# W_down's third product added in PSUM onto the fifth's sum, in a decoder layer on one core

## The chip, the core and the metric

The kernel runs on one core of one Trainium2 chip. TensorE (PE) multiplies into PSUM, VectorE (DVE) and ScalarE (ACT) work on what lies in PSUM and SBUF, GpSimd (POOL) does small things, and SyncE (SP) issues the transfers. The metric is the device time of one execution in microseconds, as the median of several runs.

## What is computed

One layer of a decoder: 512 tokens of width 1024 in fp32, with attention and convolution ahead (not touched here), then the MLP and a gated projection. Of the reference, this is the part in question:

```python
h = rms_norm(x, g_pre_mlp[i])
f = jnp.square(jax.nn.relu(h @ w_up[i])) @ w_down[i]
x = x + rms_norm(f, g_post_mlp[i])
ple_gate = jax.nn.sigmoid(rms_norm(x, g_ple[i]) @ w_ple_gate[i])
x = x + ple_gate * (p[i] @ w_ple_proj[i])
```

## The kernel before

Every fp32 operand is split into a high and a low part by `split` (lines 63 to 66: an ACT cast for the high part, a DVE subtraction for the low one), and every product is three matmuls (`mm3`, lines 90 to 93: high by high, high by low, low by high). One matmul is 128 by 128 by 512 columns.

W_down is multiplied by Strassen's method in Winograd's form: tokens are cut in an upper half (blocks 0 and 1 of 128 tokens) and a lower half (blocks 2 and 3), output columns in two halves of 512, and seven products of half size take the place of eight. They run in the order `ORDER = (1, 2, 6, 7, 5, 3, 4)`. Each product has eight tiles of weights (`i` from 0 to 7); for each tile TensorE does both token blocks `t` of a half, two slices of 128 each, so six matmuls for block 0 and then six for block 1. A sum sits in one PSUM bank per block, `acc[n, t]`. Products 6 and 5 go on in the banks of product 1 (their matmuls don't start a new sum), product 4 in those of product 7; products 1, 2, 7 and 3 start in fresh banks. There are eight banks.

At the end of a product's last tile, `done(n, t)` (lines 782 to 798) brings the sum into the column buffers `cx`, four of 128 by 1024 in SBUF: `cx[t]` for the upper tokens and `cx[t + 2]` for the lower ones. After product 5 it makes two copies of the same bank on ACT (lines 792 and 793), and the sum of product 7 and the first copy on DVE (line 794); after product 3 it adds product 3's bank to the second copy on DVE (line 796).

When a row of `cx` is complete, `chain2(t)` calls `residual1` (lines 531 to 537): the square sum of the row on ACT (`rstd_of`, L125, with an accumulator read), the row sum plus epsilon on DVE (L129), the power -1/2 on POOL (L133), the scaling by it and by the gain on DVE (L533), the addition to the residual `x` (L534), then square sum, power and scaling again for the next norm (L536). `turn(t)` transposes that row on TensorE (L141) for the gate projection. The table `AFTER` says behind which tile of which product these steps are written: block 0's chain behind product 3's last tile, block 1's behind tile 1 of product 4, block 0's transposes behind tile 5 of product 4, block 1's after the last.

TensorE and SP run in the order in which the code is written; ACT, DVE and POOL in an order that a scheduler sets by priority when the program is built, and each then runs its own list strictly in that order. The loads of the tiles (L739) are written three tiles ahead of their use, into four raw buffers; the split halves take two buffers each of a pool of 15, which also holds `cx`, the two gains (L118) and the rows that wait for their transposes. A load waits until the raw buffer's last reader, a DVE subtraction, is done. The loads of W_ple_gate (L807) for the projection share the raw buffers with the last tiles of product 4.

Of the kernel before, what the change touches and what calls it, by code (L numbers as in the profile page):

```python
# [12 lines left out]
ALU = mybir.AluOpType  # L13
# [11 lines left out]
NJ = FF // P // 2  # L25
# [8 lines left out]
def hybrid_block(ctx, tc, x, p, g_pre_mix, w_in, b_gate, w_conv, w_attn_out, w_conv_out, w_o,  # L34
                 g_post_mix, g_pre_mlp, w_up, w_down, g_post_mlp, g_ple, w_ple_gate, w_ple_proj, out):
    nc = tc.nc
# [3 lines left out]
    p = p[0]  # L40
# [13 lines left out]
    def bigt(shape, dt=F32R, name="big"):  # L54
        return big.tile(shape, dt, tag="big", name=name)

    def bank():
        return psp.tile([P, 512], F32, tag="ps", name="ps")
# [21 lines left out]
    def w4(dt=F32):  # L80
        return wts.tile([P, 2, 512], dt, tag="w", name="w4")
# [8 lines left out]
    def mm3(ps, lh, ll, rh, rl, start, stop, onto=False):  # L90
        nc.tensor.matmul(ps, lh, rh, start=start, stop=False, skip_group_check=onto)  # L91
        nc.tensor.matmul(ps, lh, rl, start=False, stop=False, skip_group_check=onto)  # L92
        nc.tensor.matmul(ps, ll, rh, start=False, stop=stop, skip_group_check=onto)  # L93
# [27 lines left out]
    def rstd_of(parts):  # L121
        ss = []
        for a in parts:
            s = sml.tile([P, 1], F32, tag="ss", name="ss")
            nc.scalar.activation(junk[:, 0:a.shape[-1]], a, AF.Square, scale=1.0 / 32.0, accum_out=s)  # L125
            ss.append(s)
        m = sml.tile([P, 1], F32, tag="ms", name="ms")
        if len(ss) == 1:
            nc.vector.tensor_scalar(m, ss[0], EPS, None, op0=ALU.add)  # L129
        else:  # L130
            nc.vector.scalar_tensor_tensor(m, ss[0], EPS, ss[1], op0=ALU.add, op1=ALU.add)
        r = sml.tile([P, 1], F32, tag="rs", name="rs")
        nc.gpsimd.tensor_tensor(r, m, mhalf, op=ALU.pow)  # L133
        return r
# [134 lines left out]
    for t in range(2, NT):  # L269
        ps = bank()  # L270
# [197 lines left out]
    for j in range(NK):  # L468
# [24 lines left out]
        if j == 7:  # L493
            for kk in range(2):
                ps = bank()
# [5 lines left out]
    def rows(nk, stat, w, tail, chain):  # L501
# [19 lines left out]
        for t in range(NT):  # L521
# [6 lines left out]
                    mm3(acc[t, hf], sh[:, tok], sl[:, tok], wk[0][:, cs], wk[1][:, cs], False, k == nk - 1)  # L528
            chain(t, [acc[t, 0], acc[t, 1]])

    def residual1(xt, c, gpost, gnext):
        r = rstd_of([c])
        nc.vector.scalar_tensor_tensor(c, c, r, gpost, op0=ALU.mult, op1=ALU.mult)  # L533
        nc.vector.tensor_tensor(xt, xt, c, op=ALU.add)  # L534
        r2 = rstd_of([xt])
        nc.vector.scalar_tensor_tensor(c, xt, r2, gnext, op0=ALU.mult, op1=ALU.mult)  # L536
        return [c[:, 0:512], c[:, 512:1024]]
# [21 lines left out]
    hf = [bigt([P, 2, 4, 256], F32, "hf") for _ in range(2)]  # L559
# [24 lines left out]
    for t in range(NT):  # L584
        tok = slice(t * P, (t + 1) * P)
        for h_ in range(2):
            cs = slice(h_ * 512, (h_ + 1) * 512)
            ps = bank()
# [142 lines left out]
    def load_t(n, i):  # L731
        raw = raws.tile([P, 2, 512], F32, tag="raw", name="raw")
        if n in RIGHT:
            r, c = RIGHT[n]
            r0 = r * FF // 2 + i * 2 * P
            src = w_down[r0:r0 + 2 * P, c * 512:(c + 1) * 512].rearrange("(k p) n -> p k n", p=P)
        else:
            src = wsum[i][:, MADE[n]]
        nc.sync.dma_start(raw, src)  # L739
        lo, hi = w4(F32R), w4(F32R)  # L740
        split(hi, lo, raw)
        for u in range(2):
            tiles[n, 2 * i + u] = hi[:, u], lo[:, u]

    def load_s(n, g):
        if (n, g) == (1, 0):
            hi, lo = (wts.tile([P, 4, 256], F32R, tag="w", name="s0") for _ in range(2))
        else:
            both = bigt([P, 2, 4, 256], name="sb")
            hi, lo = both[:, 0], both[:, 1]  # L750
        split(hi, lo, quarter(*LEFT[n], g))
        for v in range(4):
            stat[n, 4 * g + v] = hi[:, v], lo[:, v]
        a11, a12 = quarter(0, 0, g), quarter(0, 1, g)
        if n == 1:
            nc.vector.tensor_tensor(a11, quarter(1, 0, g), a11, op=ALU.subtract)
        elif n == 2:
            nc.vector.tensor_tensor(a12, a12, a11, op=ALU.subtract)
        elif n == 6:
            nc.vector.tensor_tensor(a11, quarter(1, 1, g), a11, op=ALU.subtract)  # L760

    back = {}
    xr2 = lambda t: back['x', t // 2][:, t % 2, :]
# [9 lines left out]
    cx = {}  # L773
    hn2 = {}
    h3 = []
    acc = {}

    def chain2(t):
        hn2[t] = residual1(xr2(t), cx[t].rearrange("p a b -> p (a b)"), *back["g"])

    def done(n, t):
        ps = acc[n, t]
        if n == 1:
            cx[t] = w4()
            cx[t + 2] = w4()
            nc.scalar.copy(cx[t][:, 0], ps)
        elif n == 2:
            nc.vector.tensor_tensor(cx[t][:, 0], ps, cx[t][:, 0], op=ALU.add)
        elif n == 6:
            nc.scalar.copy(cx[t + 2][:, 0], ps)  # L790
        elif n == 5:
            nc.scalar.copy(cx[t + 2][:, 1], ps)
            nc.scalar.copy(cx[t][:, 1], ps)
            nc.vector.tensor_tensor(cx[t + 2][:, 1], acc[7, t], cx[t + 2][:, 1], op=ALU.add)
        elif n == 3:
            nc.vector.tensor_tensor(cx[t][:, 1], ps, cx[t][:, 1], op=ALU.add)
        elif n == 4:
            nc.vector.tensor_tensor(cx[t + 2][:, 0], ps, cx[t + 2][:, 0], op=ALU.add)

# [10 lines left out]
    def turn(t):  # L810
        if not h3:
# [3 lines left out]
    plan_t = [(n, i) for n in ORDER for i in range(NI)]  # L815
    plan_s = [(n, g) for n in ORDER for g in range(4)]
    AFTER = {(7, 0): lambda: reload('x', x1s), (5, 6): gains, (4, 6): lambda: reload('p', pps), (3, 7): lambda: chain2(0), (4, 1): lambda: chain2(1), (4, 2): lambda: load_pg(0),
             (4, 4): lambda: load_pg(2), (4, 5): lambda: turn(0)}
    nt = ns = 0
    for n, i in plan_t:  # L820
        while ns < min(len(plan_s), plan_s.index((n, i // 2)) + 3):
            load_s(*plan_s[ns])
            ns += 1
        while nt < min(len(plan_t), plan_t.index((n, i)) + 4):
            load_t(*plan_t[nt])
            nt += 1
        for t in range(2):
            if i == 0:
                acc[n, t] = acc[{6: 1, 5: 6, 4: 7}[n], t] if n in (6, 5, 4) else bank()
            ts = slice(t * P, (t + 1) * P)  # L830
            for j in (2 * i, 2 * i + 1):
                sh, sl = stat[n, j]
                th, tl = tiles[n, j]
                mm3(acc[n, t], sh[:, ts], sl[:, ts], th, tl, j == 0 and n in (1, 2, 7, 3),
                    j == NJ - 1, n in (6, 5, 4))
            if i == NI - 1:
                done(n, t)
        if (n, i) in AFTER:
            AFTER[n, i]()
    turn(1)  # L840
    for t in range(2, NT):
        chain2(t)
        for k in range(2 * t, 2 * t + 2):
            pgw[k] = wrow(w_pg, k)
# [29 lines left out]
    for t in range(2, NT):  # L874
        for cs in CUTS[t]:
            ps = bank()[:, 0:cs.stop - cs.start]
# [31 lines left out]
```

## Time and profile before

| | us |
|---|---|
| median of 3 runs | 737.27 |
| lowest and highest | 736.19 and 740.18 |
| the profiled execution | 735.77 |
| its span, first to last instruction | 734.0 |
| TensorE busy in it | 725.5 |
| VectorE busy | 518.3 |
| ScalarE busy | 379.3 |

All times in the rows are counted from the span's start. A matmul of 512 columns starts 0.227 us after the one before it when TensorE does not wait; its row shows 0.39 us because matmuls overlap in the pipeline. A block of two slices for both token blocks, twelve matmuls, takes 2.72 us. In a timeline the square bracket at a row's end tells how long the engine was idle ahead of it and what ended that.

### The profile page before, as it was taken

Reading aid. Unit: us, or ns where it says so; the run is one execution under the profiler, and the core shown is the slowest. Engines: PE = TensorE matmul, PEld = TensorE weight load, DVE = VectorE, ACT = ScalarE, POOL = GpSimd, SP = SyncE. Lnnn points to the kernel's source line nnn. Section 1 sums busy time; section 2 is a strip of 40 time slices with the busy share of each in tenths; the row PEclk is TensorE's granted clock in tenths of the full one; section 3 lists DMA queues with packets and bytes.
Section 4 is the critical chain, followed back from the end, with each engine's and each line's share of the span. In section 5 each row is a group of like instructions: output and inputs, shape, how many; then the busy total and the mean of one; then the engine's idle time right before and its main releaser. Section 6 shows DMA issues by size and latency. Waiting matters only on the chain.

```text
span 734.0 us, 10311 instructions
## 1 busy us (share of the span) xinstructions
PE 725.5 (99%) x3976; PEld 628.9 (86%) x3976; DVE 518.3 (71%) x644; ACT 379.3 (52%) x595; POOL 93.8 (13%) x120
## 2 busy tenths in 40 slices
PE   8999999999999999999999999999999999999997
PEld 7888788888888888888899999999988888888886
DVE  6777886968555534734789988976799778269762
ACT  6245446352434323433856777756867476256431
POOL 1106061433225220001100000000000000001100
PEclk9999999999999999999999999999999999999999
DMA  8595627154999966752424445523455767577311
GB/s 315 171 303 166 184 96 225 35 200 144 290 346 328 282 217 243 250 165 72 153 92 115 116 117 142 138 66 111 147 172 185 238 223 231 179 242 268 127 57 58
DMA packets 112105, 132.29 MB, mean 180 GB/s; under 512 B 4116, under 2 KB 82744, under 8 KB 111032
## 3 DMA queue, kind: packets, MB, share of 16 engines
q1 hardware_dynamic: 111464, 127.43, 54.8%
q10 hardware_dynamic: 592, 4.20, 1.4%
q8 instruction: 31, 0.51, 0.3%
q14 instruction: 18, 0.15, 0.1%
HBM read 108.55 MB, written 23.07 MB: 179 GB/s over the span
## 4 chain that ended last, share of the span: by engine, by line
PE 96%; DVE 1%; DMA 1%; ACT 1%; issue 0%; POOL 0%; DVEq 0%; SPq 0%; ACTq 0%; POOLq 0%
PE ps L91 30%; PE ps L92 30%; PE ps L93 30%; DMA raw<-in_w_conv_out_dram 1%; PE ps L340 1%; PE ps L388 1%; PE ps L374 1%; PE ps L182 1%; DVE wlo L65 1%; PE ps L568 1%; PE ps L141 0%; PE ps L201 0%; PE ps L223 0%; ACT whi L64 0%; PE ps L497 0%
## 5 line engine op out<-in xcount | busy, mean ns | idle before, releaser
L65 DVE TENSOR_TENSOR wlo<-raw,whi 128x512 fp32r<-128x512 f32 (+1 forms) x84 | 79.2, 964 | 54.0 <-ACT whi L64 42.0
L91 PE MATMUL ps<-h1h,whi 128*128 128x512 f32 x288 | 113.3, 393 | 0.9 <-DVE st L65 0.9
L93 PE MATMUL ps<-h1h,wlo 128*128 128x512 f32 x288 | 112.2, 390 | 0.0
L92 PE MATMUL ps<-h1l,whi 128*128 128x512 f32 x288 | 112.2, 389 | 0.0
L64 ACT CAST whi<-raw 128x512 fp32r<-128x512 f32 (+1 forms) x84 | 65.4, 808 | 60.8 <-DMA raw<-in_w_in_dram 29.0
L91 PE MATMUL ps<-w,sb 128*128 128x512 f32 x216 | 84.1, 389 | 0.0
L93 PE MATMUL ps<-w,sb 128*128 128x512 f32 x216 | 84.0, 389 | 0.0
L92 PE MATMUL ps<-w,sb 128*128 128x512 f32 x216 | 84.0, 389 | 0.0
L65 DVE TENSOR_TENSOR w<-raw,w 128x1024 fp32r<-128x1024 f32 x56 | 67.7, 1221 | 21.2 <-PE ps L92 10.2
L64 ACT CAST w<-raw 128x1024 fp32r<-128x1024 f32 x56 | 58.5, 1052 | 36.1 <-PE ps L93 13.6
L133 POOL TENSOR_TENSOR rs<-ms,mhalf 128x1 f32<-128x1 f32 x20 | 14.6, 729 | 440.0 <-DVE ms L129 364.7
L91 PEld LDWEIGHTS ps<-h1h,whi 128*128 128x128 f32 x288 | 54.1, 188 | 12.5 <-DVE st L65 1.1
L93 PEld LDWEIGHTS ps<-h1h,wlo 128*128 128x128 f32 x288 | 54.1, 188 | 11.4
L92 PEld LDWEIGHTS ps<-h1l,whi 128*128 128x128 f32 x288 | 54.1, 188 | 10.9
L92 PE MATMUL ps<-h2l,us 128*128 128x256 f32 x224 | 63.4, 283 | 0.0
L91 PE MATMUL ps<-h2h,us 128*128 128x256 f32 x224 | 63.4, 283 | 0.0
L93 PE MATMUL ps<-h2h,us 128*128 128x256 f32 x224 | 63.4, 283 | 0.0
L65 DVE TENSOR_TENSOR us<-raw,us 128x1024 fp32r<-128x1024 f32 x42 | 50.7, 1220 | 7.9 <-ACT us L64 7.8
L64 ACT CAST us<-raw 128x1024 fp32r<-128x1024 f32 x42 | 43.4, 1050 | 17.1 <-PE ps L93 6.3
L93 PEld LDWEIGHTS ps<-w,sb 128*128 128x128 f32 x216 | 40.5, 188 | 8.5
L92 PEld LDWEIGHTS ps<-w,sb 128*128 128x128 f32 x216 | 40.5, 188 | 8.4
L91 PE MATMUL ps<-tb,us 128*128 128x256 f32 x168 | 47.7, 284 | 0.0
(206 smaller groups left out, 1650.8 us busy)
## 6 DMA issues: line engine op xcount, KB each, us to landing
raw<-in_w_in_dram SPq DMA_DIRECT2D x36, 512.0 KB, 7.0
w<-in_w_down_dram SPq DMA_DIRECT2D x32, 512.0 KB, 4.5
wsum<-w SPq DMA_DIRECT2D x32, 512.0 KB, 4.0
raw<-in_w_up_dram SPq DMA_DIRECT2D x32, 512.0 KB, 4.2
raw<-wsum SPq DMA_DIRECT2D x32, 512.0 KB, 5.3
raw<-in_w_down_dram SPq DMA_DIRECT2D x24, 512.0 KB, 4.1
raw<-in_w_o_dram SPq DMA_DIRECT2D x8, 512.0 KB, 5.9
raw<-in_w_ple_gate_dram SPq DMA_DIRECT2D x8, 512.0 KB, 7.1
```

Source lines behind the costliest of these rows:

```text
L64: a = nc.scalar.copy(hi, src)
L65: b = nc.vector.tensor_tensor(lo, src, hi.bitcast(F32), op=ALU.subtract)
L91: nc.tensor.matmul(ps, lh, rh, start=start, stop=False, skip_group_check=onto)
L92: nc.tensor.matmul(ps, lh, rl, start=False, stop=False, skip_group_check=onto)
L93: nc.tensor.matmul(ps, ll, rh, start=False, stop=stop, skip_group_check=onto)
L133: nc.gpsimd.tensor_tensor(r, m, mhalf, op=ALU.pow)
L182: nc.tensor.transpose(warm[:, 0:P], ident, ident)
L340: nc.tensor.matmul(ps[h][:, c0:c0 + n], st[r, a, qb * P:(qb + 1) * P], st[r, b, 0:n], start=i == 0, stop=i == 2)
L374: nc.tensor.transpose(ps[:, c0 + (qb - kb) * P:c0 + (qb - kb + 1) * P], w[:, o:o + P], ident)
L388: nc.tensor.matmul(ps[:, kb * P:S], lhs, wt[i][:, c0:c0 + n], start=(kb == 0 and i == 0), stop=(kb == NT - 1 and i == 1))
L568: nc.tensor.transpose(ps[:, i * P:(i + 1) * P], hn1[t][g][:, i * P:(i + 1) * P], ident)
```

## The change

Product 3 no longer starts a sum of its own. Its matmuls go on in the bank that holds product 5's sum (and with it products 1 and 6), so that after product 3 the bank holds the upper tokens' second column half. The second copy after product 5 and the addition after product 3 are gone. For blocks 0 and 1 the norm chain reads that half from PSUM: a new `residual0` squares the two halves by themselves, scales them by themselves into a new buffer `c` of the pool of 15, and goes on as before. Blocks 2 and 3 keep `residual1`.

```diff
+    def residual0(xt, accs, gpost, gnext):
+        r = rstd_of(accs)
+        c = w4()
+        flat = c.rearrange("p a b -> p (a b)")
+        for hf in range(2):
+            nc.vector.scalar_tensor_tensor(c[:, hf], accs[hf], r, gpost[:, hf * 512:(hf + 1) * 512],
+                                           op0=ALU.mult, op1=ALU.mult)
+        nc.vector.tensor_tensor(xt, xt, flat, op=ALU.add)
+        r2 = rstd_of([xt])
+        nc.vector.scalar_tensor_tensor(flat, xt, r2, gnext, op0=ALU.mult, op1=ALU.mult)
+        return [c[:, 0], c[:, 1]]
...
     def chain2(t):
-        hn2[t] = residual1(xr2(t), cx[t].rearrange("p a b -> p (a b)"), *back["g"])
+        if t < 2:
+            hn2[t] = residual0(xr2(t), [cx[t][:, 0], acc[3, t]], *back["g"])
+        else:
+            hn2[t] = residual1(xr2(t), cx[t].rearrange("p a b -> p (a b)"), *back["g"])
...
         elif n == 5:
             nc.scalar.copy(cx[t + 2][:, 1], ps)
-            nc.scalar.copy(cx[t][:, 1], ps)
             nc.vector.tensor_tensor(cx[t + 2][:, 1], acc[7, t], cx[t + 2][:, 1], op=ALU.add)
-        elif n == 3:
-            nc.vector.tensor_tensor(cx[t][:, 1], ps, cx[t][:, 1], op=ALU.add)
...
-                acc[n, t] = acc[{6: 1, 5: 6, 4: 7}[n], t] if n in (6, 5, 4) else bank()
+                acc[n, t] = acc[{6: 1, 5: 6, 3: 5, 4: 7}[n], t] if n in (6, 5, 3, 4) else bank()
...
-                mm3(acc[n, t], sh[:, ts], sl[:, ts], th, tl, j == 0 and n in (1, 2, 7, 3),
-                    j == NJ - 1, n in (6, 5, 4))
+                mm3(acc[n, t], sh[:, ts], sl[:, ts], th, tl, j == 0 and n in (1, 2, 7), j == NJ - 1, n not in (1, 2, 7))
```

The order of TensorE's instructions stays; which bank they write changes. At the end of product 5 and the start of product 3, TensorE before (`w4_5961` and `w4_5962` are the two halves of product 5's last tile, `w4_5979` and `w4_5980` those of product 3's first; the waits are on the last signals of the engines named):

```order
L93 MATMUL ps_5241<-w4_5962,sb_5917 128x512
L91 MATMUL ps_6053<-w4_5980,sb_5956 128x512 [waits Activation_49]
L92 MATMUL ps_6053<-w4_5979,sb_5956 128x512 [waits DVE_49]
L93 MATMUL ps_6053<-w4_5980,sb_5956 128x512
L91 MATMUL ps_6053<-w4_5980,sb_5956 128x512
L92 MATMUL ps_6053<-w4_5979,sb_5956 128x512
L93 MATMUL ps_6053<-w4_5980,sb_5956 128x512
L91 MATMUL ps_6060<-w4_5980,sb_5956 128x512
```

The same place on TensorE after the change:

```order
L93 MATMUL ps_5241<-w4_5962,sb_5917 128x512
L91 MATMUL ps_5234<-w4_5980,sb_5956 128x512 [waits Activation_49]
L92 MATMUL ps_5234<-w4_5979,sb_5956 128x512 [waits DVE_49]
L93 MATMUL ps_5234<-w4_5980,sb_5956 128x512
L91 MATMUL ps_5234<-w4_5980,sb_5956 128x512
L92 MATMUL ps_5234<-w4_5979,sb_5956 128x512
L93 MATMUL ps_5234<-w4_5980,sb_5956 128x512
L91 MATMUL ps_5241<-w4_5980,sb_5956 128x512 [waits Activation_49]
```

Product 3 now writes the two banks that product 5 has just left (`ps_5234` for block 0, `ps_5241` for block 1), and its first matmul for block 1 has a wait on ACT that it did not have.

ACT at the same place before (`w4_6023` is the high half of product 3's third tile, the copies are `done(5, t)`):

```order
L64 CAST w4_6001<-raw_5998 128x1024 [waits DMAHW6_49,PE_49]
L792 COPY w4_5381<-ps_5234 128x512 [waits PE_49]
L793 COPY w4_5380<-ps_5234 128x512
L64 CAST w4_6023<-raw_6020 128x1024 [waits DMAHW1_49,DVE_49]
L792 COPY w4_5390<-ps_5241 128x512 [waits PE_49]
L793 COPY w4_5389<-ps_5241 128x512
```

ACT there after the change:

```order
L64 CAST w4_6001<-raw_5998 128x1024 [waits DMAHW6_49,PE_49]
L807 COPY w4_5381<-ps_5234 128x512 [waits PE_49]
L64 CAST w4_6023<-raw_6020 128x1024 [waits DMAHW1_49,DVE_49]
L807 COPY w4_5390<-ps_5241 128x512 [waits PE_49]
L64 CAST w4_6048<-raw_6045 128x1024 [waits DMAHW2_49,DVE_49]
```

One copy of each pair is gone; the cast that waits for a load still stands between block 0's copy and block 1's.

ACT in the last tiles of product 4 before (`w4_6279`, `w4_6307` and `w4_6325` are the high halves of tiles 5, 6 and 7 of product 4, `pgh` those of W_ple_gate; `junk` rows are the squares, of `x` or of a row of `cx`):

```order
L64 CAST w4_6279<-raw_6276 128x1024 [waits DMAHW4_49,PE_49,Activation_49]
L64 CAST pgh_6295<-raw_6300 128x1024 [waits DMAHW6_49]
L125 ACTIVATE junk_90,ss_6212<-x_5739 128x1024 [waits DVE_49,Activation_49]
L125 ACTIVATE junk_90,ss_6258<-w4_5389 128x1024 [waits Activation_49]
L64 CAST w4_6307<-raw_6304 128x1024 [waits DMAHW7_49,PE_49]
L64 CAST w4_6325<-raw_6322 128x1024 [waits DMAHW0_49,PE_49]
L64 CAST pgh_6341<-raw_6342 128x1024 [waits DMAHW1_49]
L64 CAST pgh_6341<-raw_6346 128x1024 [waits DMAHW2_49]
L125 ACTIVATE junk_90,ss_6266<-x_5739 128x1024 [waits DVE_49,Activation_49]
```

ACT there after the change (tiles 5, 6 and 7 are `w4_6281`, `w4_6309` and `w4_6327`; `ps_5241` is the bank of block 1):

```order
L125 ACTIVATE junk_90,ss_6210<-x_5739 128x1024 [waits DVE_49,Activation_49]
L125 ACTIVATE junk_90,ss_6256<-w4_5389 128x512 [waits Activation_49]
L125 ACTIVATE junk_90,ss_6258<-ps_5241 128x512 [waits PE_49,Activation_49]
L64 CAST pgh_6297<-raw_6302 128x1024 [waits DMAHW6_49]
L64 CAST w4_6281<-raw_6278 128x1024 [waits DMAHW4_49,PE_49]
L64 CAST w4_6309<-raw_6306 128x1024 [waits DMAHW7_49,PE_49]
L64 CAST pgh_6343<-raw_6344 128x1024 [waits DMAHW1_49]
L125 ACTIVATE junk_90,ss_6268<-x_5739 128x1024 [waits DVE_49,Activation_49]
L64 CAST w4_6327<-raw_6324 128x1024 [waits DMAHW0_49]
L64 CAST pgh_6343<-raw_6348 128x1024 [waits DMAHW2_49]
```

The squares of the first `x` and of block 1 now stand ahead of the second W_ple_gate cast and of tile 5, and the cast of tile 7 stands behind the third W_ple_gate cast and the square of the second `x`, where it stood ahead of both.

## Rows read from the trace of the kernel before

**Rows 1.** The page: busy time by engine, and the chain that ended last.
```profile
PE 725.5 (99%) x3976; PEld 628.9 (86%) x3976; DVE 518.3 (71%) x644; ACT 379.3 (52%) x595; POOL 93.8 (13%) x120
...
PE 96%; DVE 1%; DMA 1%; ACT 1%; issue 0%; POOL 0%; DVEq 0%; SPq 0%; ACTq 0%; POOLq 0%
```

**Rows 2.** Windows: stretch, length, busy time by engine, granted clock, DMA share, GB/s.
```profile
600.00:638.00 38.00, 38.00 (x169) 31.49 (x168) 24.94 (x23) 20.43 (x22) 0.00 (x0) 1.00 0.60 186
...
665.00:690.00 25.00, 25.00 (x120) 20.88 (x119) 20.84 (x25) 12.93 (x20) 3.58 (x4) 1.00 0.68 253
690.00:710.00 20.00, 20.00 (x98) 16.49 (x96) 16.60 (x26) 10.81 (x21) 1.96 (x3) 1.00 0.07 27
710.00:734.00 24.00, 19.74 (x110) 17.15 (x108) 6.63 (x12) 2.56 (x5) 0.00 (x0) 0.96 0.18 66
```

**Rows 3.** ACT's timeline at product 5's end: start, length, line, operation, tiles.
```profile
637.34 0.59 ACT L792 COPY w<-ps 128x512 f32<-128x512 f32 x1 [8.46 <-PE ps L93]
...
640.18 1.05 ACT L64 CAST w<-raw 128x1024 fp32r<-128x1024 f32 x1 [1.77 <-DMA raw<-in_w_down_dram]
641.14 0.58 ACT L792 COPY w<-ps 128x512 f32<-128x512 f32 x1
```

**Rows 4.** Groups by line and form: count, busy us, mean ns, idle before.
```profile
L125 ACT ACTIVATE junk<-ps 128x512 bf16<-128x512 f32 x8 | 4.9, 606 | 4.2 <-PE ps L93 4.1
L125 ACT ACTIVATION_READ_ACCUMULATOR junk<-ps 128x1 f32 x8 | 1.6, 206 | 0.0
L125 ACT ACTIVATE junk<-w 128x1024 bf16<-128x1024 f32 x4 | 4.2, 1058 | 5.1 <-DVE w L798 4.0 <-DVE w L796 1.0
...
L544 DVE SCALAR_TENSOR_TENSOR tmp<-ps,rs,gb 128x512 f32<-128x512 f32 x8 | 5.6, 746 | 2.4 <-POOL rs L133 2.4
```

**Rows 5.** Timelines of ACT and DVE at the end of product 2.
```profile
573.46 1.05 ACT L64 CAST w<-raw 128x1024 fp32r<-128x1024 f32 x1 [1.01 <-PE ps L93]
...
573.85 0.69 DVE L788 TENSOR_TENSOR w<-ps,w 128x512 f32<-128x512 f32 x1
```

**Rows 6.** TensorE's timeline at the start of product 3.
```profile
638.50 0.39 PE L91 MATMUL ps<-w,sb 128*128 128x512 f32 x1
...
639.86 0.39 PE L91 MATMUL ps<-w,sb 128*128 128x512 f32 x1
```

**Rows 7.** SP's timeline of issues; then raw's landings from 615 to 690 us.
```profile
633.46 11.34 SPq L739 DMA_DIRECT2D raw<-in_w_down_dram  x6
...
658.82 3.05 SPq L807 DMA_DIRECT2D raw<-in_w_ple_gate_dram  x2
...
668.76 1.56 SPq L807 DMA_DIRECT2D raw<-in_w_ple_gate_dram  x2
...
DMA to landing us min/median/max: 3.7/5.5/9.7
```

**Rows 8.** Timelines of DVE and ACT in the upper norm chain.
```profile
659.10 0.69 DVE L796 TENSOR_TENSOR w<-ps,w 128x512 f32<-128x512 f32 x1 [0.30 <-PE ps L93]
...
662.90 1.28 DVE L533 SCALAR_TENSOR_TENSOR w<-w,rs,gb 128x1024 f32<-128x1024 f32 x1 [0.73 <-POOL rs L133]
...
663.13 1.05 ACT L64 CAST pgh<-raw 128x1024 fp32r<-128x1024 f32 x1 [1.21 <-DMA raw<-in_w_ple_gate_dram]
...
665.79 1.06 ACT L64 CAST pgh<-raw 128x1024 fp32r<-128x1024 f32 x1 [0.66 <-DMA raw<-in_w_ple_gate_dram]
...
674.64 1.05 ACT L64 CAST pgh<-raw 128x1024 fp32r<-128x1024 f32 x1 [0.89 <-DMA raw<-in_w_ple_gate_dram]
```

**Rows 9.** The chain that ended last, in order of time: the transposes.
```profile
676.75 0.88 PE ps L141 x8
683.08 0.87 PE ps L141 x8
```

**Rows 10.** Waits of the weight loads from 625 us on: total, times, longest.
```profile
PEld ps L92 <- DVE wlo L65: 0.2, 1, 0.2
```

**Rows 11.** TensorE's timeline at the longest idle stretch within its work.
```profile
80.13 0.50 PE L91 MATMUL ps<-h1h,whi 128*128 128x512 f32 x1 [0.88 <-DVE st L65]
```

## The prediction

> **What bounds the kernel now.** I read the page first, then windows of the last third, then the engines' timelines around the two places that the diff touches. The page says that TensorE is busy 99% of the span and that 96% of the chain that ended last is TensorE's [rows 1]. The windows say the same of the stretch that matters: from 600 us to 710 us, the second half of W_down and the start of the gate projection (of the windows one is left out, 638 to 665 us, equally full), TensorE is busy for every microsecond, at the granted clock 1.00, while DVE and ACT have idle time [rows 2]. So work taken from ACT or DVE is worth nothing by itself, and any wait put on TensorE is paid in full, because no later idle time is there to absorb it. The question is only whether the change makes TensorE wait.
>
> **What is removed and added on ACT and DVE.** Removed: per upper token block one PSUM copy of 0.59 us on ACT and one PSUM add of 0.69 us on DVE [rows 3, 8]. The single square of 1.06 us becomes two halves of 0.61 us, each with its accumulator read, so ACT gains about 0.4 us per block; the scaling of 1.28 us becomes two halves of 0.75 us on DVE [rows 4, 8]. All of it lies beside TensorE: the net cost is nothing as long as the two queues stay ahead, and even in the fullest stretch, 665 to 690 us, DVE has 20.84 and ACT 12.93 us of work in 25 [rows 2]. The scaled row takes a buffer of its own from the pool of 15 that the tiles use; four column buffers, two gains and four tiles in flight take 14, so it is the fifteenth, and costs nothing. One half square (block 0, finished after the second product) stands early in ACT's queue, waiting for the add that began at 573.85 us; the cast behind it, now at 573.46 us, moves to about 575.3 us [rows 5]. It prepares the seventh tile of product 6, which TensorE reaches only six blocks of 2.72 us later. Cost nothing.
>
> **The new wait, term A.** Product 3 used to write two fresh banks; now its first matmul for each token block must wait until ACT has copied product 5's sum out of the same bank. Product 5 is directly ahead in the order, so the cover is only the other block's six matmuls, 6 x 0.227 = 1.36 us.
> Block 0: its copy ran 637.34 to 637.93 us, and product 3's first matmul for it starts at 638.50 us [rows 3, 6]. No wait.
> Block 1: its copy did not start when TensorE finished product 5 (its last matmul is the one before 638.50 us) but at 641.14 us [rows 3, 6]. It stands on ACT behind a cast that waits for a W_down tile, product 3's third, whose transfer was issued at 633.46 us, after the two gain loads, and let the cast start at 640.18 us, 6.7 us later [rows 3, 7]. In the changed kernel the cast is still ahead of this copy. The copy ends at 641.14 + 0.59 = 641.73 us, the signal takes some 0.03 us, and the first matmul for block 1, now at 639.86 us [rows 6], starts at about 641.76 us: **A = 1.90 us**. Behind the waiting matmul stands everything on TensorE. ACT does not wait in turn: it only needs product 5.
> Bounds of A: it moves one for one with the landing. Transfers of this stage took 3.7 to 9.7 us, median 5.5 [rows 7]. The copy can at the earliest start with the end of product 5, which hides it, so the lower end is 0, and a wait cannot be a gain; at the longest, 9.7 us, A is 4.9 us. I take the row's own 1.90, since it is the same transfer behind the same gain loads.
> The Trainium skill, PSUM — Partial Sum Buffer, section "PSUM bank collisions raise a hardware error", says that no two engines may be in one bank at once and that access must be guarded bank by bank. By that rule the wait cannot be left away even where the words copied and written would differ; without it A would be 0 and the sum 0.7 us instead of 2.6. No run here shows the collision; the order of the changed kernel shows the wait.
>
> **The upper norm chain, term B.** Block 0's accumulation ends 1.90 us later than the 659.10 us at which the removed add began [rows 8], about 661.0. From there: half square with accumulator read 0.82, row sum 0.15, power 0.73 from the sum to the scaling, two halves 1.5 us: 664.2 us, the time at which the present chain also gets there (662.90 + 1.28) [rows 4, 8]. So the chain loses nothing in absolute time, and the transposes of block 0 at 676.75 us [rows 9] have as much room as before or more. But the order behind it changes on ACT: both half squares of block 1 now stand ahead of the second W_ple_gate cast, and the cast of product 4's last tile now stands behind the third W_ple_gate cast and behind the square of x, where it was ahead of both.
> Step by step: square of x at 666.5, done with its read 667.7; two half squares 1.64 to 669.3; the second W_ple_gate cast 1.05 to 670.4 (it began at 665.79 [rows 8]); its DVE half, behind one scaling, to about 671.8. That frees the buffer for the third W_ple_gate load, issued at 668.76 us now [rows 7], so 3.0 us later. It took until 674.64 us, 5.9 us, while the first took 4.3 us (658.82 to 663.13) [rows 7, 8]: landing between 676.1 and 677.7 us. Then ACT has that cast, the square of x and the last tile's cast, and DVE has the low half of W_ple_gate, row sum, the power's 0.73 us, the scaling of 1.28 us and the last tile's low half of 1.22 us: from landing to the end of that low half 5.5 us. TensorE needs it one matmul into the last block: 683.08 (transposes of block 1) - 2.72 + 0.23 = 680.59 [rows 9], plus the 1.90 of A: 682.5 us. Lateness is landing + 5.5 - 682.5: 0 at the early landing, 0.7 at the late one, and 1.2 if the chain slips another half microsecond. The third load now has less beside it, which speaks for the early side: **B = 0.5 us**, ends 0 and 1.2.
>
> **The last norm chain, term C.** At 698 us a weight load already waits 0.2 us for the low half of a W_ple_gate tile, so there is no room there [rows 10]. The change puts the row sum of block 3, and with it the power's 0.73 us round trip, between the fourth and the sixth of these halves, where only the fifth covers part of it. **C = 0.2 us**, ends 0 and 0.4.
>
> **Sum.** A + B + C = 1.9 + 0.5 + 0.2 = 2.6 us, all on TensorE's path. The profiled execution took 735.77 us, 734.0 of it span; with the change 738.4 us. The median of the three runs is 737.27 us, 1.5 us above it, so the forecast is 739.9 us, 0.35% up. A measurement of this kernel can tell about 0.5% (3.7 us) from no change, so this counts as the same.
>
> **The rivals.** *No stall:* the product 3 tile lands before about 637.9 us, 4.4 us after issue, and the copy of block 1 runs in the cover. For it: other W_down and wsum transfers land in that time [rows 7]. Against: this one shares the queues with a gain load. Then B and C remain at most: 737.3 to 738.0 us. Chance 0.12.
> *The wait grows:* the same cast waits longer. From a landing 7.8 us after issue, A passes 3.0 and the sum 3.7 us, the point from which it is slower; at 9.7 us the time is 737.27 + 4.9 + 0.7 = 742.9. For it: 9.7 us occurs in this stage; also B at its upper end needs only A = 2.3. Against: 6.7 us was measured. Chance 0.27.
> *The clock falls:* a stall lets TensorE drop to its lower level. The longest idle stretch inside the present program, 0.88 us before 80.13 us, kept the clock at 1.00; in the last window, where TensorE is done for some microseconds, the mean is 0.96, so the lower level does come back after idle time [rows 2, 11]. At 1.2 GHz instead of 2.4 each block of 2.72 us costs 2.72 us more; two blocks give 739.9 + 5.4 = 745.3 us. Chance 0.05.
> The Trainium skill, TensorE: Matmul & The Clock Gate, section "Why this matters for your kernels", warns of idle gaps between bursts of matmuls for this reason; by it a stall much longer than A would end in this rival. The trace shows no gap as long as A, and no run here decides it yet.
> *Faster:* the shorter ACT and DVE queues end a wait. TensorE idles nowhere from 600 to 710 us to a hundredth [rows 2], so nothing over 0.5% can come back: 737 us. Chance 0.04, mostly for the spread of the runs.
>
> **How the numbers follow.** The forecast has 0.52 and no stall 0.12, both within 0.5%: same 0.64. The grown wait and the clock are slower: 0.32. Faster 0.04. The range runs from no stall less 0.4 us for the spread of the runs, 736.9 us, to the grown wait at its longest, 742.9 us; it leaves out the clock and the ends beyond, some 0.15.
>
> **What would show it.** Right: in the profile after, TensorE has an idle stretch of 1 to 3 us at about 639.9 us, ended by an ACT copy that stands behind a cast waiting for a W_down load; the banks of product 3 cause no wait for block 0; a second gap of up to 1.2 us ended by DVE stands in the last block of product 4, some 3 us ahead of block 1's transposes. Wrong: no gap at 640 us (the tile landed early), a granted clock below 1.00 behind the gap, or a gap elsewhere of more than 1.5 us.

## The result

The changed kernel takes 738.99 us (median of 20 runs, 736.87 to 741.95), the kernel before 736.76 us (20 runs, 735.29 to 741.17): a ratio of 1.0027, with a 95% interval of 1.0015 to 1.0039. By the ratio that is 2.0 us more, 1.1 to 2.9 by the interval (the two medians lie 2.23 us apart): within half a per cent, and yet clearly not nothing. The forecast was 2.6 us more.

The profiled execution of the changed kernel took 739.33 us, 737.6 of it span, 3.6 us more span than before. Not all of that belongs to the change: 1.6 us of it are there already when TensorE reaches the transposes at 358 us (358.61 us here, 357.01 before), in code that the change does not touch. Nearly all of that is the wait of [rows 11], here 2.58 us long where it was 0.88 before:

```profile
81.98 0.50 PE L91 MATMUL ps<-h1h,whi 128*128 128x512 f32 x1 [2.58 <-DVE st L65]
```

The profiles of the experiments scatter at the transposes by 3 us too. From those transposes to the start of the last matmul it is 372.45 us before and 374.44 after: 1.99 us, which agrees with the medians. This stretch is used below as the second measure, beside the medians.

TensorE's busy time on the page of the profile after, which answers to [rows 1]:

```profile
PE 726.6 (99%) x3976; PEld 629.4 (85%) x3976; DVE 516.3 (70%) x644; ACT 378.0 (51%) x597; POOL 93.6 (13%) x120
```

DVE and ACT have 2.0 and 1.3 us less to do, and the kernel is slower all the same. The windows of the same profile show where TensorE lost time (columns as in [rows 2]: stretch, length, busy time by engine, granted clock, DMA share, GB/s):

```profile
600.00:638.00 38.00, 38.00 (x169) 31.51 (x168) 26.56 (x23) 21.29 (x22) 0.00 (x0) 1.00 0.58 181
638.00:665.00 27.00, 25.57 (x113) 20.84 (x113) 13.26 (x14) 12.38 (x15) 0.55 (x1) 1.00 0.75 248
665.00:690.00 25.00, 25.00 (x120) 20.87 (x119) 21.49 (x26) 14.50 (x22) 3.04 (x4) 1.00 0.74 279
690.00:713.00 23.00, 23.00 (x110) 18.80 (x109) 18.05 (x28) 11.85 (x22) 1.95 (x3) 1.00 0.06 24
```

Only in the second row is TensorE's busy time, the first figure behind the length, below the length: 1.43 us are missing, where before every microsecond was full. TensorE's timeline there shows the last matmul for block 0, the first for block 1 (which [rows 6] has at 639.86 us) and the one behind it:

```profile
641.23 0.39 PE L93 MATMUL ps<-w,sb 128*128 128x512 f32 x1
643.05 0.50 PE L91 MATMUL ps<-w,sb 128*128 128x512 f32 x1 [1.43 <-ACT w L807]
643.39 0.39 PE L92 MATMUL ps<-w,sb 128*128 128x512 f32 x1
```

From start to start 1.82 us pass instead of 0.227, so the wait costs 1.59 us (the 1.43 us of the row count from the pipelined end of the matmul before), and the first matmul behind it takes 0.34 us to the next start, 0.11 more. It is product 3's first matmul for block 1. ACT's timeline, beside [rows 3]:

```profile
638.94 0.59 ACT L807 COPY w<-ps 128x512 f32<-128x512 f32 x1 [8.46 <-PE ps L93]
641.47 1.04 ACT L64 CAST w<-raw 128x1024 fp32r<-128x1024 f32 x1 [1.95 <-DMA raw<-in_w_down_dram]
642.42 0.58 ACT L807 COPY w<-ps 128x512 f32<-128x512 f32 x1
```

ACT idles 1.95 us for a tile of W_down while block 1's finished sum waits in the same queue, and the copy that frees the bank ends at 643.00 us, 0.05 us ahead of the matmul. The chain that ended last, in order of time (start, length, what), goes through just these four pieces; before, it was TensorE alone here:

```profile
635.07 6.33 DMA raw<-in_w_down_dram
641.47 1.04 ACT w L64
642.51 0.49 ACT w L807
643.05 0.50 PE ps L91
```

The waits of TensorE and of its weight loads from 625 us on (us in total, times, longest) show one more, which [rows 10] had at 0.2:

```profile
PE ps L91 <- ACT w L807: 1.4, 1, 1.4
...
PEld ps L92 <- DVE wlo L65: 0.4, 1, 0.4
```

At this one of the last low halves of W_ple_gate, start to start is 0.39 us, so 0.16 us are lost.

### The profile page after: what moved, and what is told of

It is laid out like the page before. It is cut to its first block, busy times and chain, and to the rows that moved or that the text cites. A ratio compares the mean times of both kernels' runs of the same rounds, so it can differ in the third digit from the quotient of the medians.

```text
span 737.6 us, 10316 instructions
## 1 busy us (share of the span) xinstructions
PE 726.6 (99%) x3976; PEld 629.4 (85%) x3976; DVE 516.3 (70%) x644; ACT 378.0 (51%) x597; POOL 93.6 (13%) x120
## 4 chain that ended last, share of the span: by engine, by line
PE 71%; DMA 2%; DVE 2%; POOL 1%; ACT 1%; SPq 0%; issue 0%; ACTq 0%
PE ps L92 23%; PE ps L91 23%; PE ps L93 23%; DMA raw<-in_w_in_dram 2%; DMA raw<-in_w_down_dram 1%; PE ps L580 1%; DVE wlo L65 0%; POOL beta L351 0%; PE ps L141 0%; DVE w L309 0%; ACT whi L64 0%; SPq L303 0%; DVE wtl L65 0%; POOL keep L351 0%; DVE beta L355 0%
```

## The experiments

All were compared with the kernel before on the same chip. A, B and C are the places of the prediction, and the waits are read from TensorE's timeline, start to start less 0.227 us: A at product 3's first matmul for block 1, B in product 4's sixth and last tiles, C at the low halves of W_ple_gate. "Clock" is what matmuls at the lower clock took longer. "Stretch" is the time from the transposes at 357 us to the last matmul's start, less the 372.45 us of before.

| kernel | median, before beside it | ratio (95%) | A | B | C | clock | stretch |
|---|---|---|---|---|---|---|---|
| changed | 738.99, 736.76 | 1.0027 (1.0015 to 1.0039) | 1.59 | 0 | 0.16 | 0 | +1.99 |
| changed, again | 737.69, 735.92 | 1.0029 (1.0012 to 1.0045) | 1.58 | 0 | 0.30 | 0 | +2.10 |
| copy first | 736.04, 735.92 | 0.9993 (0.9978 to 1.0008) | 0 | 0 | 0.40 | 0 | +0.43 |
| bank alone | 738.73, 735.92 | 1.0040 (1.0025 to 1.0055) | 1.72 | 0 | 0.80 | 0 | +2.75 |
| bank held, eight | 742.26, 735.92 | 1.0081 (1.0053 to 1.0109) | 4.28 | 0 | 0.16 | 1.6 | +6.25 |
| chain alone | 738.92, 736.42 | 1.0028 (1.0014 to 1.0042) | 0 | 0.61 | 1.93 | 0 | +2.97 |
| gains later | 737.34, 736.42 | 1.0012 (0.9997 to 1.0028) | 0 | 0.77 | 0.59 | 0 | +1.74 |
| chain alone, weights first | 736.73, 735.79 | 1.0018 (1.0004 to 1.0032) | 0 | 0.58 | 0 | 0 | +0.78 |
| copy and weights first | 735.79, 735.79 | 1.0001 (0.9990 to 1.0013) | 0 | 0 | 0 | 0 | +0.03 |
| bank held, six | 741.09, 735.79 | 1.0074 (1.0056 to 1.0093) | 3.04 | 0 | 0.16 | 1.6 | +5.02 |

The waits of a row add up to its stretch within 0.5 us (each restart behind a wait costs another 0.1), and each stretch, as a share of 736 us, lies inside the interval of its ratio.

**The changed kernel again**, beside the others on their chip.

> The changed kernel once more, beside its variants on the same chip. All theories: 1.002 to 1.004 of before. Theory 1 (the wait for the bank): TensorE idles 1.4 to 2.0 us ahead of product 3's first matmul for block 1, ended by ACT's copy; the gap's length follows the landing of product 3's third tile, one for one. Rival (the norm chain or the shared bank by itself costs the time): the gap is there or not, but the difference to before sits elsewhere.

1.0029, with the same wait of 1.58 us in the same place. The result repeats.

**Copy first.** The split of product 3's third tile is put behind block 1's copy in ACT's order; nothing else is meant to change.

```diff
-    def load_t(n, i):
+    def load_t(n, i, behind=None):
...
-        split(hi, lo, raw)
+        if behind is None:
+            split(hi, lo, raw)
+        else:
+            with tc.issue_after(behind.ins):
+                split(hi, lo, raw)
...
-            nc.scalar.copy(cx[t + 2][:, 1], ps)
+            copied[t] = nc.scalar.copy(cx[t + 2][:, 1], ps)
```

> The changed kernel with one thing undone on ACT: the cast of product 3's third tile is put behind the copy of block 1's bank, so that the copy no longer waits for a load. Theory 1: no idle time of TensorE at the start of product 3, the copy starts within 0.3 us of product 5's last matmul, and the time falls by 1.6 us against the changed kernel, to 1.000 to 1.001 of before. Rival (the chain or the accumulation costs it): the gap goes, but the time stays at 1.002 to 1.004.

0.9993 (0.9978 to 1.0008): the loss is gone, but for the 0.40 us of C in the stretch. ACT's timeline shows the swap:

```profile
638.55 0.59 ACT L812 COPY w<-ps 128x512 f32<-128x512 f32 x1 [0.77 <-PE ps L93]
639.69 1.05 ACT L64 CAST w<-raw 128x1024 fp32r<-128x1024 f32 x1 [0.55 <-DMA raw<-in_w_down_dram]
```

The copy now starts when TensorE finishes block 1's sum, and the cast still waits for its transfer, but with nothing behind it that anyone needs. The window from 638 us is full again:

```profile
638.00:665.00 27.00, 27.00 (x121) 22.36 (x120) 16.82 (x17) 14.59 (x16) 0.55 (x1) 1.00 0.73 245
```

So the wait was not the price of sharing the bank; it was the place of the copy in ACT's queue.

**Gains later.** The other way to the same end: the two gains are loaded behind tile 4 of product 3 instead of ahead of its tiles, so that product 3's tiles come earlier. The scheduler then also puts the third tile's cast ahead of both copies: it is done before product 5 ends.

```diff
-    AFTER = {(7, 0): lambda: reload('x', x1s), (5, 6): gains, ...
+    AFTER = {(7, 0): lambda: reload('x', x1s), (3, 4): gains, ...
```

> The changed kernel with the two gain loads issued behind tile 4 of product 3 in place of behind tile 6 of product 5, so that product 3's third tile no longer queues behind them. Theory 1: that tile lands before product 5 ends, the casts ahead of the copies find it there, and the gap at product 3's start is 0 to 0.5 us; 1.000 to 1.001 of before, unless the later gains delay the norm chain, which shows as a wait in product 4's last tiles (up to 1.5 us). Rival (the gap is from the copy or the bank, not from the load): the gap stays at 1.4 us or more.

1.0012 (0.9997 to 1.0028). The wait at product 3 is gone here too, but two others take part of its place, at the sixth tile of product 4 (tile 5, with 0.08 us more at the last tile) and at the last low halves of W_ple_gate. TensorE's timeline at the first, and DVE's ahead of it:

```profile
673.70 0.39 PE L91 MATMUL ps<-w,sb 128*128 128x512 f32 x1
674.62 0.50 PE L92 MATMUL ps<-w,sb 128*128 128x512 f32 x1 [0.53 <-DVE w L65]
```

```profile
656.95 3.79 DVE L65 TENSOR_TENSOR w<-raw,w 128x1024 fp32r<-128x1024 f32 x3 [9.19 <-ACT w L64]
660.65 0.15 DVE L131 SCALAR_TENSOR_TENSOR ms<-ss 128x1 f32<-128x1 f32 x1
...
672.02 0.75 DVE L536 SCALAR_TENSOR_TENSOR w<-w,rs,gb 128x512 f32<-128x512 f32 x1 [0.73 <-POOL rs L133]
672.69 0.75 DVE L536 SCALAR_TENSOR_TENSOR w<-ps,rs,gb 128x512 f32<-128x512 f32 x1
673.35 1.22 DVE L65 TENSOR_TENSOR w<-raw,w 128x1024 fp32r<-128x1024 f32 x1
```

The tile's low half stands behind block 1's two scalings and ends at 674.57 us. In the changed kernel it stands there too, ends at 676.56 us, and the matmul that reads it starts at 677.41 us: 0.85 us to spare. One could think that the stall at product 3 bought this time. The copy-first kernel, which has no stall, says no; DVE's and TensorE's timelines there:

```profile
659.67 0.16 DVE L131 SCALAR_TENSOR_TENSOR ms<-ss 128x1 f32<-128x1 f32 x1 [1.03 <-ACT junk L125]
...
671.86 1.22 DVE L65 TENSOR_TENSOR w<-raw,w 128x1024 fp32r<-128x1024 f32 x1
```

```profile
673.93 0.39 PE L92 MATMUL ps<-w,sb 128*128 128x512 f32 x1
```

The half ends at 673.08 us and its reader starts at 673.93 us: the same 0.85 us. So this edit made the wait itself. The issue of the first gain now waits on SP for 9.4 us until TensorE is done with a matmul, and product 4's first loads stand behind the gains: they go out from 649.64 us, where the copy-first kernel has 644.72. DVE then does three low halves in a row, and block 0's row sum behind them starts at 660.65 us, 1 us later than in the copy-first kernel, with everything that follows it, while TensorE without the wait would be at the tile at the same 673.93 us.

**The bank alone.** Product 3 accumulates in product 5's bank, but its sum is copied to `cx` by ACT and all four blocks use the old chain.

```diff
-        if t < 2:
-            hn2[t] = residual0(xr2(t), [cx[t][:, 0], acc[3, t]], *back["g"])
-        else:
-            hn2[t] = residual1(xr2(t), cx[t].rearrange("p a b -> p (a b)"), *back["g"])
+        hn2[t] = residual1(xr2(t), cx[t].rearrange("p a b -> p (a b)"), *back["g"])
...
+        elif n == 3:
+            nc.scalar.copy(cx[t][:, 1], ps)
```

> One part alone: product 3 goes on in product 5's bank, but the finished half is copied to the row in SBUF and the old norm chain is kept for all blocks. Theory 1: the same gap of 1.4 to 2.0 us, 1.002 to 1.003 of before. Rival (the new chain is the cost): no more than 1.001.

1.0040 (1.0025 to 1.0055). TensorE waits at the same matmul, for the same copy:

```profile
642.41 0.50 PE L91 MATMUL ps<-w,sb 128*128 128x512 f32 x1 [1.56 <-ACT w L804]
```

So A belongs to the bank and not to the chain. The ratio is above the 1.002 to 1.003 that was expected, because C is 0.80 us here. DVE's order at these halves is that of the changed kernel, and the half that is waited for ends at 702.49 us (702.45 there), but TensorE would be at it 0.6 us earlier, at 701.75 instead of 702.35 us. So the same order costs more or less by how far TensorE is ahead.

**The chain alone.** The kernel before, with the changed kernel's `residual0` for blocks 0 and 1, reading two halves of `cx` in SBUF; product 3 keeps its own banks.

```diff
+            hn2[t] = residual0(xr2(t), [cx[t][:, 0], cx[t][:, 1]], *back["g"])
```

> The other part alone: product 3 keeps banks of its own and the copy and addition of before, but blocks 0 and 1 take the new chain (two half squares, two half scalings into a new buffer), reading both halves from SBUF. Theory 1: no gap at the start of product 3, 0.999 to 1.001 of before, if the new order on ACT and DVE stays covered. Theory 2 (terms B and C of the prediction): TensorE waits for the low half of product 4's last tile or of the last W_ple_gate tiles, 0.5 to 4 us in all, 1.001 to 1.005. Rival (the chain is the cost of the change): 1.002 to 1.004 with the gaps spread.

1.0028 (1.0014 to 1.0042): as much as the whole change, with no wait at product 3 at all. The waits of TensorE from 625 us on:

```profile
PE ps L92 <- DVE wlo L65: 1.6, 1, 1.6
PE ps L92 <- DVE w L65: 0.3, 1, 0.3
```

DVE's timeline at the longer one:

```profile
698.07 1.90 DVE L65 TENSOR_TENSOR wlo<-raw,whi 128x512 fp32r<-128x512 f32 x3
699.88 0.15 DVE L129 TENSOR_SCALAR ms<-ss 128x1 f32<-128x1 f32 x1
700.76 1.28 DVE L548 SCALAR_TENSOR_TENSOR w<-x,rs,gb 128x1024 f32<-128x1024 f32 x1 [0.73 <-POOL rs L133]
701.97 0.68 DVE L65 TENSOR_TENSOR wlo<-raw,whi 128x512 fp32r<-128x512 f32 x1
```

Of eight halves seven are through at 699.88 us, and the last stands behind the row sum, POOL's power (0.73 us of idle DVE) and the scaling of block 3: 2.1 us. In the changed kernel the same scaling stands behind all eight. The two parts of the change, each by itself, thus cost 2.75 and 2.97 us of stretch, and together 1.99: they don't add.

**The chain alone, with the weights first.** The chain-alone kernel, with the last four rows of W_ple_gate split ahead of block 3's chain.

```diff
-    for t in range(2, NT):
-        chain2(t)
-        for k in range(2 * t, 2 * t + 2):
-            pgw[k] = wrow(w_pg, k)
+    chain2(2)
+    for k in range(4, 8):
+        pgw[k] = wrow(w_pg, k)
+    chain2(3)
```

> The chain-alone kernel again (own banks for product 3, the chain of the upper blocks reads two halves), with one thing changed: all four rows of W_ple_gate that come after block 1's transposes are loaded and split ahead of block 3's norm chain, so on DVE no low half stands behind block 3's scaling. Theory (order on DVE): the wait of 1.72 us at the last low half and the 0.20 us before it are gone, the 0.60 us in product 4's last tiles stays: about 1.9 us less than the chain-alone kernel, which took 738.92 against 736.42 us; ratio to the kernel before 1.0010, TensorE without any gap at these halves. Rival (the half waits for its transfer, or DVE has too much work in all): the gap stays at 1.5 us or more and the ratio at 1.003.

1.0018 (1.0004 to 1.0032), and a stretch of +0.78 where the chain alone had +2.97. The ratio lies above the 1.0010 that was expected, which is in the interval. The halves now stand in one row on DVE, and no wait for them is left on TensorE:

```profile
696.37 3.70 DVE L65 TENSOR_TENSOR wlo<-raw,whi 128x512 fp32r<-128x512 f32 x6
699.98 1.22 DVE L546 TENSOR_TENSOR x<-x,w 128x1024 f32<-128x1024 f32 x1
```

So C was here the order on DVE, not the transfers and not the amount of work. B stays, at 0.58 us.

**Copy and weights first.** Both repairs on the changed kernel: the edits of the copy-first kernel and of the one just above.

> The changed kernel with block 1's copy ahead of the waiting cast on ACT and with the late W_ple_gate rows split ahead of block 3's norm chain: both places where TensorE still waited are cleared. Theory (the whole cost of the change is these waits, and nothing else is gained or lost): no gap on TensorE behind 600 us, ratio 0.999 to 1.001. Rival (the shorter ACT and DVE work ahead of the gate projection is worth something once no wait hides it): ratio below 0.998. Rival (block 3's chain, now behind the halves, makes the transposes of block 3 late): a new gap behind 700 us, ratio above 1.001.

1.0001 (0.9990 to 1.0013), both medians 735.79 us. Its windows have no idle time on TensorE:

```profile
638.00:665.00 27.00, 27.00 (x121) 22.36 (x120) 16.83 (x17) 14.50 (x16) 0.55 (x1) 1.00 0.71 236
665.00:690.00 25.00, 25.00 (x120) 20.86 (x119) 20.14 (x26) 13.41 (x23) 3.04 (x4) 1.00 0.69 266
690.00:710.00 20.00, 20.00 (x98) 16.57 (x97) 16.58 (x25) 10.21 (x20) 1.65 (x3) 1.00 0.07 27
```

The change without its waits costs nothing and brings nothing: the copies and additions that it removes were hidden before. From 638 to 710 us TensorE has no gap to give back, so there is nothing here for another version of this change to win.

**The bank held.** The copy-first kernel, with eight idle copies of block 1's bank on ACT ahead of the needed one; they add work and leave out none.

```diff
-            nc.scalar.copy(cx[t + 2][:, 1], ps)
+            for _ in range(8 * t):
+                nc.scalar.copy(junk[:, 0:512], ps)
+            copied[t] = nc.scalar.copy(cx[t + 2][:, 1], ps)
```

> The variant with the copy first, but with eight idle copies of block 1's bank (0.48 us each) ahead of the needed one, so that the bank is held about 3.9 us longer. Theory 1, every microsecond of the wait is paid in full: a gap of 4.0 to 4.5 us, time 4.0 to 4.5 us over the variant with the copy first, 1.005 to 1.007 of before, granted clock 1.00 throughout. Rival (the clock falls in a stall of this length): granted clock below 1.00 in the windows behind the gap and 6 us or more over the variant with the copy first. Rival (later slack takes it back): the gap is there and the time rises by less than 2 us.

1.0081 (1.0053 to 1.0109), some 6 us, more than the wait of 4.28 us: the first theory, with the clock at 1.00 throughout, is wrong, and the rival on the clock holds. TensorE's timeline shows the rest:

```profile
641.69 0.39 PE L93 MATMUL ps<-w,sb 128*128 128x512 f32 x1
646.20 0.50 PE L91 MATMUL ps<-w,sb 128*128 128x512 f32 x1 [4.12 <-ACT w L814]
...
647.38 0.63 PE L92 MATMUL ps<-w,sb 128*128 128x512 f32 x1
647.81 0.63 PE L93 MATMUL ps<-w,sb 128*128 128x512 f32 x1
...
650.64 0.39 PE L91 MATMUL ps<-w,sb 128*128 128x512 f32 x1
```

Behind the gap some matmuls start 0.43 us apart instead of 0.227, as at 1.2 GHz in place of 2.4; then they are 0.227 us apart again. It makes 1.6 us in all. The window has the granted clock below 1.00, for the first time in this stage:

```profile
638.00:665.00 27.00, 22.88 (x94) 18.44 (x94) 11.09 (x10) 15.42 (x21) 0.00 (x0) 0.94 0.63 215
```

**The bank held by six copies**, to see whether a shorter wait keeps the clock.

```diff
-            for _ in range(8 * t):
+            for _ in range(6 * t):
```

> The copy-first kernel with six idle copies of block 1's bank on ACT ahead of the needed one, where the bank-held kernel had eight; they add work and leave out none. With eight, TensorE waited 4.28 us from start to start less a matmul, and the granted clock fell 0.8 us behind the gap: eight matmuls at 0.43 instead of 0.227 us, 1.6 us more. Each idle copy took 0.61 us, so the wait is 3.1 us here. Theory A (any wait of some us brings the lower clock): 3.1 + 1.6 us and 0.4 at the last halves, ratio 1.006 to 1.007. Theory B (the clock holds at this length): 3.1 + 0.4 us, ratio 1.004 to 1.005, every matmul behind the gap 0.227 us apart.

1.0074 (1.0056 to 1.0093): theory A's 1.006 to 1.007 lies in the interval, theory B's 1.004 to 1.005 does not. TensorE idles 2.89 us, and again the matmuls behind it are 0.43 us apart, from the second on:

```profile
642.47 0.55 PE L91 MATMUL ps<-w,sb 128*128 128x512 f32 x1 [2.89 <-ACT w L814]
642.82 0.63 PE L92 MATMUL ps<-w,sb 128*128 128x512 f32 x1
643.25 0.63 PE L93 MATMUL ps<-w,sb 128*128 128x512 f32 x1
...
645.81 0.58 PE L93 MATMUL ps<-w,sb 128*128 128x512 f32 x1
```

But that any wait of this length brings the lower clock does not hold in general. The wait of [rows 11], in code that all these kernels share, was 2.58 us in the changed kernel's first profile, and the granted clock stayed at 1.00; in its second profile it was 2.37 us, and the clock fell. TensorE's timeline and window there:

```profile
82.14 0.50 PE L91 MATMUL ps<-h1h,whi 128*128 128x512 f32 x1 [2.37 <-DVE st L65]
```

```profile
60.00:90.00 30.00, 27.63 (x126) 22.71 (x125) 23.35 (x26) 12.16 (x24) 11.11 (x16) 0.94 0.55 165
```

## Why the prediction held, point by point

**What bounds the kernel.** Right. Every wait on TensorE came out in the time, and the work taken from ACT and DVE brought nothing; the copy-and-weights-first kernel shows both at once. (The 0.4 us per block that ACT was to gain come to 0.2 by the prediction's own rows, and to 0.65 by the pages, 1.3 for both; nothing hangs on it.)

**Term A.** Right in place, cause and order, a little too large: 1.90 us forecast, 1.59 measured (1.70 with the slow restart). The step was that the wait moves one for one with the landing of product 3's third tile. From its issue at 635.07 us to the cast at 641.47 us it took 6.4 us, where [rows 3, 7] gave 6.7; that is the whole difference. The copy-first kernel, which has the same transfer and no wait, shows that the queue is the cause. That block 0 does not wait was right: its copy ended at 639.53 us, and product 3's first matmul started at 640.10 us.

The Trainium skill, PSUM — Partial Sum Buffer, section "PSUM bank collisions raise a hardware error", asks for a guard for every bank that two engines share. The trace agrees so far as it shows the guard at work, the wait of TensorE for ACT's copy out of the same bank; no run here shows a collision.

**Term B.** 0.5 us forecast, 0 measured, within its ends of 0 and 1.2. The step that was mis-sized is the landing of the third W_ple_gate tile. SP's and ACT's timelines after:

```profile
673.60 3.32 SPq L819 DMA_DIRECT2D raw<-in_w_ple_gate_dram  x2
```

```profile
677.49 1.06 ACT L64 CAST pgh<-raw 128x1024 fp32r<-128x1024 f32 x1 [3.12 <-DMA raw<-in_w_ple_gate_dram]
```

It took 3.9 us, below both the 4.3 and the 5.9 us between which the prediction chose. The last tile's low half was then in time by 0.57 us: it ended at 683.18 us, and its reader started at 683.75. What the prediction did not see is a second place in product 4 that is nearly as tight: the sixth tile's low half has moved behind block 1's scalings and is in time by 0.85 us, with the stall A or without it, as the copy-first kernel shows. The chain-alone and gains-later kernels, whose block 0 starts its row sum later, pay 0.45 and 0.69 us at it, and 0.15 and 0.08 us more at the last tile, where the prediction had looked.

**Term C.** Right: 0.2 us forecast, 0.16 measured, 0.30 when repeated. That norm-chain work between the halves is the cause was argued from the order, and the two weights-first kernels show it: with the halves ahead, C is 0. They move the row sum, the power, the scaling and an addition together, so which of these it is they don't show. That the size came out so well is in part luck: the kernels with this same order on DVE have 0.16 to 0.80 us.

**The sum.** 2.6 us forecast; A, C and the restart make 1.86, the stretch 1.99, and the medians 2.0 (1.1 to 2.9). The time in microseconds, 739.9, is 0.9 above the measured 739.0: 0.4 because the medians are 2.2 us apart and not 2.6, and 0.5 because the median of before was 737.27 in three runs and is 736.76 in twenty.

**The rivals.** *No stall* is excluded by the wait. *The wait grows* did not happen in the two profiles taken, whose waits are 1.59 and 1.58 us. But its long end was priced too low: in both bank-held kernels a wait of 3.0 or 4.3 us brought the lower clock with it, 1.6 us more, so a wait of 4.9 us would by this estimate have made 744.5 us and not 742.9. *The clock falls* did not happen at A's size; with longer waits it did, and its price was put too high, 5.4 us for two blocks at 1.2 GHz, where the traces show 1.6. The Trainium skill, TensorE: Matmul & The Clock Gate, section "Why this matters for your kernels", warns of idle gaps between bursts of matmuls. The traces agree: behind an idle gap of 1.43 us the granted clock stays at 1.00, behind 2.89 and 4.12 us it is lower for a while; in between they are divided, with 1.00 behind 2.58 us and a lower clock behind 2.37 us. *Faster* is excluded by the copy-and-weights-first kernel.

**One thing was left out of the working:** what the shared bank does for the new chain. The prediction counts the removed additions as worth nothing by themselves. In the chain-alone kernel both are still there, 0.69 us each on DVE ahead of block 0's row sum, which starts at 661.17 us, where the copy-first kernel, with TensorE 0.26 us earlier, has 659.67. That is 1.2 us later, more than the 0.85 us that the sixth tile's half had to spare. So the new chain alone costs as much as the whole change, and the parts don't add. This is read from the timelines; no kernel here takes the additions away alone.

## What to carry to other kernels

When a sum goes on in a bank that another engine still has to empty, look at what stands ahead of the emptying copy in that engine's queue, not at the copy's own length: 0.6 us of copy cost 1.6 us of TensorE because a cast ahead of it waited for a transfer, and putting the copy first took that wait away. Look through the whole profile after a repair: loading the gains later ended the same wait, but held up the loads behind them and made another wait 35 us on. The parts of a change measured alone need not add: here 2.75 and 2.97 us apart, 1.99 together. And the work taken from engines that are not the bound brought nothing: the best version of this change equals the kernel before.

## What was not expected of the hardware

The lower clock cost about the same whenever it came, and far less than a whole stage at half speed: behind idle gaps of 2.89 and 4.12 us on TensorE the matmuls lost 1.6 us more each time, behind one of 1.43 us nothing. With the shorter of the two the matmuls were slow from the second on, with the longer one from the fourth on (0.8 us later). The length of the gap does not settle it alone: one of 2.37 us brought the lower clock and one of 2.58 us at the same place did not. What decides it, no run here shows.
